# Token mixers of a two-block network: branch order, convolution taps and a reciprocal table

## The chip, the core and the metric

One core of a Trainium2 chip runs the whole program. The metric is the device time of one execution in microseconds, taken as the median of several runs. Five engines work side by side, each through a list of instructions of its own, in order: TensorE (PE, its weight loads are PEld), VectorE (DVE), ScalarE (ACT), GpSimd (POOL) and SyncE (SP, which issues most DMAs). They wait for each other through semaphores.

## What is computed

Two blocks follow each other on 256 tokens of width 1024. The change lies in the first one, which has two layers. Each layer runs a token mixer and a gated feed-forward net; in layer 0 also 256 context tokens go through it (512 columns in all), in layer 1 the 256 tokens alone ask, with keys and values of the context. The mixer has three branches, each closed by a projection and a gate:

```python
u = h @ w_glu                                   # convolution branch, 512 channels
u = u[..., :512] * sigmoid(u[..., 512:])
u = depthwise_conv(u, conv_w, conv_b)           # 31 taps
y_a = silu(layer_norm(u, ln_g, ln_b)) @ w_conv_out

q, k, v = diff_qkv(h, w_q, w_k, w_v)            # 8 heads, two score sets each
p = softmax(q k / 8)                            # both sets
o = (p[:, :, 0] - lam * p[:, :, 1]) @ v
y_b = rms_norm(o) * (1 - lam_init) @ w_attn_out

p = h @ w_p                                     # pool branch, windows 2, 4, 8, 16
y_c = (groupwise(window_mean(p) - p, w_group) * scale) @ w_pool_out

g = sigmoid(h @ w_g + b_gate)                   # three gates of 1024
y = (g[0] * y_a + g[1] * y_b + g[2] * y_c) @ w_out
```

Beside that, `silu(c) @ w_mod + b_mod` gives shifts and scales of every layer, and the second block, which is not touched, starts from an rms norm of 256 memory tokens (`mem_norm`).

## The kernel before

All activations lie transposed, 128 channels by the tokens, in tiles of a common ring (`slot`, SLOTS = 66 tiles of 128x512); the convolution's and the pool's padded inputs have a ring of their own (`u_tile`, US = 6). Each float32 product is made as three matmuls of split operands, hi by hi, hi by lo and lo by hi (`mm3`, L164 to L166). A weight piece is loaded by SP, ScalarE writes its high part (`whi`, L154) and VectorE, for some pieces GpSimd, subtracts the low part (`wlo`, L155); four pieces of each may be in use. PSUM has six buffers for products (`p`) and two for transposes and small sums (`tr`).

`mixer1` (L747) makes a list of steps, each with a cost. `merge(main, side)` spreads the side steps evenly over the main ones by cost, and `emit` runs the list in that order. This order is the priority of a scheduler, which then sorts the instructions of each engine by when their inputs and buffers are due; a step that needs no new buffer can come earlier than its place, one that takes a slot hardly can.

The steps of a mixer in the kernel before, by the stages of which the text speaks:
- projections of the gated convolution input, then queries, keys and values of head pair 0, with the first 20 of 124 convolution taps beside them;
- four attention stages: the projections of the next head pair (in the fourth: the gate of the convolution branch, `gates(0)`) merged with the attention of the current pair (`att_s` scores and softmax, `att_t` transposes, `att_v` values) and 26 taps each. A tap (`conv_tap`) of channel tiles 0 and 1 is one VectorE instruction (L795), one of tiles 2 and 3 a scaling on ScalarE into a slot (L792) and an addition on GpSimd (L793). The first 62 taps belong to tiles 0 and 2 (the first group), the others to tiles 1 and 3 (the second);
- `o_fin`, which finishes the heads' scale factors; the pool projection (4 tiles) merged with the layer norm of the convolution, `conv_ln` (sums), `conv_ln2` (root and broadcast), `conv_ln3` (four tiles);
- `b1`, the convolution's output product (8 tiles, evacuated on VectorE by `merge_a`, L947), merged with the window sums (`pool_win`);
- `gates(2)`, the gate of the pool branch, in layer 0 merged with the first seven parts of a modulation product that VectorE makes (`mod_v`, L476 and L478, its weights `mraw` loaded half a megabyte at a time into two buffers), in layer 1 with `mem_norm(0)`;
- `groups`, the pool's small group products (L1010, L1011 evacuate them), and `b3`, its output product, added by `merge_c` (L952, addition on GpSimd L953);
- `b2`, the attention's gate and output products in turn, with the transposes of the finished heads (`o_tr`, L1031 to L1035) at its start and the rest of the modulation behind; then the mixer's output product.

`att_s` takes the reciprocals of both softmax sums into a small tile (L856) and copies the first of them into a table V["Ri"] (L860), where `o_fin` finds it.

## Time and profile before

| | us |
|---|---|
| median of 3 runs | 2349.7 |
| the runs | 2348.4, 2349.7, 2353.44 |
| span of the profiled execution | 2355.8 |
| TensorE busy | 2197.7 (93%) |
| VectorE busy | 1707.7 (72%) |
| ScalarE busy | 1095.3 (46%) |
| GpSimd busy | 536.5 (23%) |

The profile shows one execution; its span is 6.1 us longer than the median. The mixer of layer 0 lies at about 107 to 610 us, that of layer 1 at 1117 to 1431 us. In the tables of stages, TensorE's idle time is the length of a stage less TensorE's busy time, and PEclk is the clock that TensorE was granted as a share of the full one (2.4 GHz; 0.5 of it is the lower level of 1.2 GHz). Idle time of the other engines costs nothing as long as TensorE does not wait for them.

### The profile page before, as it was taken

What the parts mean: (1) busy time and instruction counts of PE and PEld (TensorE: products, weight loads), DVE (VectorE), ACT (ScalarE), POOL (GpSimd) and SP (SyncE); (2) the same over time, 40 slices, a digit from 0 to 9 for tenths busy, and PEclk for the clock granted to TensorE, in tenths of its full rate; (3) what the DMA queues carried; (4) which work ended last, traced back from release to release, by engine and by line L of the source; (5) the groups of instructions that cost most, each with busy time, mean ns of one, the idle gap of its engine ahead of it and who ended that gap; (6) DMA issues with size and microseconds to landing.
All of it is one profiled execution on the core that took longest, in us unless ns stands there. A gap on an engine that the chain in (4) does not pass through costs nothing.

```text
span 2355.8 us, 37801 instructions
## 1 busy us (share of the span) xinstructions
PE 2197.7 (93%) x14576; PEld 1998.8 (85%) x14576; DVE 1707.7 (72%) x3443; ACT 1095.3 (46%) x2110; POOL 536.5 (23%) x545
## 2 busy tenths in 40 slices
PE   4978889999989999989999899999889999999998
PEld 3767777788888888878788899999877999988998
DVE  5697987959678745578988877764686766686665
ACT  5436565332332222244566554554446544465543
POOL 2344433321340110143333312100342000210000
PEclk8989999999999999998999999999987999999999
DMA  7312112335414555553322454455541555542553
GB/s 271 93 55 67 54 59 72 123 132 170 152 63 154 168 179 170 170 165 108 108 72 90 148 174 160 154 193 176 160 90 37 176 183 177 177 144 84 185 180 125
DMA packets 296628, 319.21 MB, mean 135 GB/s; under 512 B 20544, under 2 KB 264352, under 8 KB 296448
## 3 DMA queue, kind: packets, MB, share of 16 engines
q1 hardware_dynamic: 293072, 311.27, 41.1%
q0 software_dynamic: 2224, 3.43, 0.6%
q8 instruction: 114, 1.87, 0.3%
q10 hardware_dynamic: 1152, 2.10, 0.3%
q14 instruction: 66, 0.54, 0.1%
HBM read 315.72 MB, written 1.05 MB: 134 GB/s over the span
## 4 chain that ended last, share of the span: by engine, by line
PE 66%; DVE 21%; issue 4%; ACT 3%; DMA 3%; POOL 1%; SPq 0%; ACTq 0%; DVEq 0%; POOLq 0%
PE p L164 19%; PE p L165 19%; PE p L166 19%; DVE wlo L155 3%; DVE t L795 3%; DVE t L478 2%; DVE t L258 2%; PE p L742 1%; DVE b L851 1%; DMA mraw<-in_w_mod_dram 1%; DVE t L725 1%; PE tr L484 1%; DMA raw<-in_w_in_dram 1%; PE p L247 1%; ACT whi L154 1%
## 5 line engine op out<-in xcount | busy, mean ns | idle before, releaser
L164 PE MATMUL p<-t,whi 128*128 128x256 f32 (+1 forms) x3724 | 1175.5, 320 | 20.8 <-ACT t L560 8.5
L165 PE MATMUL p<-t,whi 128*128 128x256 f32 (+1 forms) x3724 | 1183.0, 319 | 5.6 <-DVE t L561 2.1
L166 PE MATMUL p<-t,wlo 128*128 128x256 f32 (+1 forms) x3724 | 1178.2, 318 | 6.4 <-DVE wlo L155 4.8
L164 PEld LDWEIGHTS p<-t,whi 128*128 128x128 f32 x3724 | 718.8, 195 | 72.6 <-ACT t L560 10.3
L165 PEld LDWEIGHTS p<-t,whi 128*128 128x128 f32 x3724 | 723.6, 194 | 50.8 <-DVE t L659 3.5
L166 PEld LDWEIGHTS p<-t,wlo 128*128 128x128 f32 x3724 | 723.1, 194 | 50.4 <-DVE wlo L155 5.9
L154 ACT ACTIVATE whi<-raw 128x1024 fp32r<-128x1024 f32 (+4 forms) x487 | 492.0, 1020 | 543.4 <-PE p L165 332.6
L155 DVE TENSOR_TENSOR wlo<-raw,whi 128x1024 fp32r<-128x1024 f32 (+4 forms) x443 | 545.4, 1232 | 201.7 <-ACT whi L154 113.7
L155 POOL TENSOR_TENSOR wlo<-raw,whi 128x1024 fp32r<-128x1024 f32 (+2 forms) x44 | 103.5, 2353 | 503.6 <-ACT whi L154 464.8
L478 DVE SCALAR_TENSOR_TENSOR t<-mraw,big,t 128x512 f32<-128x512 f32 x224 | 176.6, 827 | 17.7 <-DMA mraw<-in_w_mod_dram 16.2
L793 POOL TENSOR_TENSOR t<-t,t 128x512 f32<-128x512 f32 (+1 forms) x120 | 134.9, 1125 | 186.0 <-ACT t L792 178.5
L594 POOL TENSOR_TENSOR t<-t,t 128x256 f32<-128x256 f32 (+1 forms) x68 | 70.4, 1063 | 246.1 <-ACT t L596 242.8
L299 POOL TENSOR_TENSOR t<-t,t 128x256 f32<-128x256 f32 (+1 forms) x27 | 25.6, 948 | 430.6 <-ACT t L297 430.1
L260 ACT ACTIVATE t<-t 128x256 fp32r<-128x256 f32 (+1 forms) x115 | 54.3, 473 | 148.9 <-DVE t L689 104.4
L742 PE MATMUL p<-t,t 64*128 64x256 f32 (+2 forms) x528 | 78.5, 374 | 28.5 <-DVE t L261 9.8
L247 PE MATMUL p<-whi,t 128*128 128x256 f32 x352 | 101.8, 289 | 2.8 <-ACT t L853 1.6
L248 PE MATMUL p<-wlo,t 128*128 128x256 f32 x352 | 99.8, 284 | 0.0
L249 PE MATMUL p<-whi,t 128*128 128x256 f32 x352 | 99.8, 283 | 0.0
L689 DVE TENSOR_TENSOR t<-t,p 128x256 f32<-128x256 f32 (+1 forms) x91 | 43.1, 474 | 76.8 <-PE p L166 76.6
L795 DVE SCALAR_TENSOR_TENSOR t<-u,big,t 128x512 f32<-128x512 f32 (+1 forms) x120 | 94.9, 791 | 1.5
L742 PEld LDWEIGHTS p<-t,t 64*128 64x128 f32 x528 | 50.9, 206 | 49.2 <-issue 16.8
L257 ACT ACTIVATE t<-t 128x256 fp32r<-128x256 f32 (+1 forms) x92 | 43.2, 495 | 100.0 <-DVE t L725 80.6
(299 smaller groups left out, 2717.0 us busy)
## 6 DMA issues: line engine op xcount, KB each, us to landing
raw<-in_w_in_dram SPq DMA_DIRECT2D x60, 1024.0 KB, 5.1
raw<-in_l_w_gate_up_dram SPq DMA_DIRECT2D x44, 1024.0 KB, 5.1
raw<-in_w_ffn_in_dram SPq DMA_DIRECT2D x42, 1024.0 KB, 5.3
mraw<-in_w_mod_dram SPq DMA_DIRECT2D x80, 512.0 KB, 4.0
raw<-in_l_w_in_dram SPq DMA_DIRECT2D x15, 1024.0 KB, 5.2
raw<-in_l_w_down_dram SPq DMA_DIRECT2D x16, 896.0 KB, 4.9
t<-in_w_mod_dram SPq DMA_DIRECT2D x32, 256.0 KB, 5.4
raw<-in_w_attn_out_dram SPq DMA_DIRECT2D x8, 1024.0 KB, 5.2
```

The source lines that it names most:

```text
L154: nc.scalar.activation(p.hi, src, AF.Copy)
L155: eng.tensor_tensor(p.lo, src, p.hi, op=ALU.subtract)
L164: mm(ps, lh, rh, start=first, stop=False)
L165: mm(ps, lh, rl, start=False, stop=False)
L166: mm(ps, ll, rh, start=False, stop=last)
L247: mm(ps[:, :256], lh, p.hi[:, k % 4], start=k == 0, stop=False)
L248: mm(ps[:, :256], lh, p.lo[:, k % 4], start=False, stop=False)
L249: mm(ps[:, :256], ll, p.hi[:, k % 4], start=False, stop=k == 7)
L478: nc.vector.scalar_tensor_tensor(acc, w[:, k], c, acc, op0=ALU.mult, op1=ALU.add)
L742: self.nc.tensor.matmul(out[half], q[i // 2][h, qs], k[i % 2][h, ks], start=i == 0, stop=i == 2)
L793: nc.gpsimd.tensor_tensor(acc, acc, t, op=ALU.add)
L795: nc.vector.scalar_tensor_tensor(acc, u, w, acc, op0=ALU.mult, op1=ALU.add)
```

## The change

The three branches are added in another order, pool first, then convolution, then attention, and the side steps stand beside other main steps. The first addition (now of the pool) writes V["m"], the convolution's adds to it on GpSimd, the attention's still comes last. The gates' tiles are keyed by branch, since two gates are now alive together. The attention stages get 17, 17, 17 and 23 taps, the fourth has `gates(2)` beside it; 11 taps each go beside the pool projection and the first four tiles of `gates(0)`, the rest beside the pool's output product. The softmax reciprocals are written straight into a table of twice the size and the copy goes.

```diff
-SLOTS, RING, MORE, RAWS, US, MRAWS = 66, 4, 4, 2, 6, 2
+SLOTS, RING, MORE, RAWS, US, MRAWS = 64, 4, 4, 2, 7, 2
...
-        V["Ri"] = self.const([128, 8 * nq], self.nm("Ri"))
+        V["Ri"] = self.const([128, 16 * nq], self.nm("Ri"))
...
-            r = self.brief([128, 2])
+            j = hd * nq + t
+            r = V["Ri"][:, 2 * j:2 * j + 2]
             nc.vector.reciprocal(r, L)
...
-            j = hd * nq + t
-            nc.vector.tensor_copy(V["Ri"][:, j:j + 1], r[:, 0:1])
...
-            V["gt", m] = t
+            V["gt", br, m] = t
...
-        def merge_a(m, ps):
-            t = V.pop(("gt", m))
+        def merge_c(m, ps):
+            t = V.pop(("gt", 2, m))
...
             V["m", m] = t
-        def merge_c(m, ps):
-            t = V.pop(("gt", m))
+        def merge_a(m, ps):
+            t = V.pop(("gt", 0, m))
...
-        out += merge(qkv(0), conv[:20])
-        ncv = len(conv) - 20
+        taps = iter(conv)
+        take = lambda n: [t for _, t in zip(range(n), taps)]
+        out += merge(qkv(0), take(17))
         for pr in range(4):
-            main = qkv(pr + 1) if pr < 3 else gates(0)
-            side = att(pr)
-            out += merge(merge(main, side), conv[20 + pr * ncv // 4: 20 + (pr + 1) * ncv // 4])
-        out.append(X(o_fin))
+            main = qkv(pr + 1) if pr < 3 else gates(2)
+            out += merge(merge(main, att(pr)), take(17 if pr < 3 else 23))
         pl = []
         self.lin(pl, W, 4096, 512, hx, N, pool_evac)
+        out += merge(pl, take(11) + [X(o_fin)])
+        rest = [X(lambda m=m: pool_win(m)) for m in range(4)]
+        if l == 1:
+            rest.append(X(lambda: self.mem_norm(0)))
+        g0 = gates(0)
+        out += merge(merge(g0[:4], rest), take(11))
+        gr = groups()
+        b3 = []
+        self.lin(b3, a["w_pool_out"][l], 0, 1024, lambda: V["z"], N, merge_c, K=4)
+        out += gr + merge(b3, list(taps))
         side = [X(conv_ln), X(conv_ln2)] + [X(lambda m=m: conv_ln3(m)) for m in range(4)]
-        out += merge(pl, side)
+        out += merge(g0[4:], side, 1)
         b1 = []
         self.lin(b1, a["w_conv_out"][l], 0, 1024, lambda: V["u3"], N, merge_a, K=4)
-        out += merge(b1, [X(lambda m=m: pool_win(m)) for m in range(4)])
+        ms = []
         if l == 0:
-            ms = []
             self.mod_v(ms, 0, (4, 5, 8, 9, 6, 7), 2)
-            out += merge(gates(2), ms[:8])
-        else:
-            out += merge(gates(2), [X(lambda: self.mem_norm(0))])
-        out += groups()
-        b3 = []
-        self.lin(b3, a["w_pool_out"][l], 0, 1024, lambda: V["z"], N, merge_c, K=4)
-        out += b3
+        out += merge(b1, ms[:12])
...
-        out += merge(b2[:2], [X(lambda h=h: o_tr(h)) for h in range(8)]) + (merge(b2[2:], ms[8:]) if l == 0 else b2[2:])
+        out += merge(b2[:2], [X(lambda h=h: o_tr(h)) for h in range(8)]) + merge(b2[2:], ms[12:])
```

Outside the two mixers the order of every engine stays. Inside, three places are shown as the scheduler leaves them. Comments are removed too, so that line numbers differ by one or two.

VectorE at the end of the third attention stage of layer 0, before. L155 is a weight subtraction, L258 the low half of a value tile, L887 the reduction of a finished head, L795 a tap, and L851 the row maxima of the fourth stage's first scores:

```order
L155 TENSOR_TENSOR wlo_3153<-raw,whi_3152 128x1024
L258 TENSOR_TENSOR t_3137<-p_3112,t_3137 128x2x128
L887 TENSOR_REDUCE t_2991<-tr_3143 128x128
L795 SCALAR_TENSOR_TENSOR t_2269<-u_802,big,t_2269 128x512
L155 TENSOR_TENSOR wlo_3242<-raw,whi_3241 128x1024
L851 TENSOR_REDUCE b_1313<-p_3192 128x1
L851 TENSOR_REDUCE b_1313<-p_3193 128x1
L851 TENSOR_REDUCE b_1313<-p_3210 128x1
L851 TENSOR_REDUCE b_1313<-p_3211 128x1
L856 RECIPROCAL b_1313<-b_1313 128x2
```

The same place in the changed kernel (L886 is the reduction):

```order
L155 TENSOR_TENSOR wlo_3069<-raw,whi_3068 128x1024
L258 TENSOR_TENSOR t_3053<-p_3028,t_3053 128x2x128
L886 TENSOR_REDUCE t_2912<-tr_3059 128x128
L795 SCALAR_TENSOR_TENSOR t_2841<-u_802,big,t_2841 128x512 x7
L851 TENSOR_REDUCE b_1305<-p_3107 128x1
L851 TENSOR_REDUCE b_1305<-p_3108 128x1
L851 TENSOR_REDUCE b_1305<-p_3125 128x1
L851 TENSOR_REDUCE b_1305<-p_3126 128x1
```

Before, one tap stands between the reduction and the maxima, and the taps end soon after; now seven stand there, and more of the second group's follow in the fourth stage, while the first group's in the first stage keep their places.

VectorE in layer 0, where the first split of the transposed heads (L1035) comes, before. L952 is the last merge of the pool product:

```order
L952 SCALAR_TENSOR_TENSOR t_4457<-t_4457,p_4630 128x512
L155 TENSOR_TENSOR wlo_4646<-raw,whi_4645 128x1024
L155 TENSOR_TENSOR wlo_4749<-raw,whi_4748 128x1024
L1035 SCALAR_TENSOR_TENSOR t_4677<-tr_4692,big,t_4676 128x512
L1035 SCALAR_TENSOR_TENSOR t_4679<-tr_4703,big,t_4678 128x512
L1035 SCALAR_TENSOR_TENSOR t_4681<-tr_4714,big,t_4680 128x512
L1035 SCALAR_TENSOR_TENSOR t_4683<-tr_4725,big,t_4682 128x512
L1035 SCALAR_TENSOR_TENSOR t_4685<-tr_4736,big,t_4684 128x512
```

The same in the changed kernel. L951 is the merge of a convolution output tile, L478 a modulation multiply and add on `mraw` weights:

```order
L951 SCALAR_TENSOR_TENSOR t_4409<-t_4409,p_4618 128x512
L155 TENSOR_TENSOR wlo_4640<-raw,whi_4639 128x1024
L478 SCALAR_TENSOR_TENSOR t_4586<-mraw_4612,big,t_4586 128x512
L478 SCALAR_TENSOR_TENSOR t_4587<-mraw_4612,big,t_4587 128x512
```

and further on, behind five more of L478:

```order
L478 SCALAR_TENSOR_TENSOR t_4587<-mraw_4633,big,t_4587 128x512
L1035 SCALAR_TENSOR_TENSOR t_4671<-tr_4686,big,t_4670 128x512
L1035 SCALAR_TENSOR_TENSOR t_4673<-tr_4697,big,t_4672 128x512
L155 TENSOR_TENSOR wlo_4743<-raw,whi_4742 128x1024
L155 TENSOR_TENSOR wlo_4807<-raw,whi_4806 128x1024
L1035 SCALAR_TENSOR_TENSOR t_4675<-tr_4708,big,t_4674 128x512
```

Before, merges and weight subtractions alone stand ahead of the splits; now 38 of L478 and 6 of L476 stand between the last convolution normalisation and the first L1035.

ScalarE in layer 1, ahead of the evacuation of the pool groups, before. L909 is a gate tile, L1010 the groups' evacuation:

```order
L909 ACTIVATE t_12866<-p_12841,big 128x256
L154 ACTIVATE whi_12868<-raw 128x1024
L154 ACTIVATE whi_12900<-raw 128x1024
L909 ACTIVATE t_12897<-p_12872,big 128x256
L1010 ACTIVATE t_12904<-p_12908,big 128x256
L1010 ACTIVATE t_12904<-p_12914,big 128x256
L154 ACTIVATE whi_12932<-raw 128x1024
L1010 ACTIVATE t_12906<-p_12920,big 128x256
L1010 ACTIVATE t_12906<-p_12926,big 128x256
```

The same in the changed kernel. L908 is the gate tile, L792 the scaling of a tap, L1308 the squares of the memory tokens, L1330 the high halves of the normalised memory, L1009 the groups' evacuation:

```order
L908 ACTIVATE t_12397<-p_12372,big 128x256
L792 ACTIVATE t_12399<-u_9853,big 128x256
L154 ACTIVATE whi_12528<-raw 128x1024
L1308 ACTIVATE t_12412,c_12411<-t_12403 128x512
L1308 ACTIVATE t_12414,c_12411<-t_12405 128x512
L1308 ACTIVATE t_12416,c_12411<-t_12407 128x512
L1308 ACTIVATE t_12418,c_12411<-t_12409 128x512
L1330 ACTIVATE t_12471<-t_12448,big 128x256 x2
L1330 ACTIVATE t_12473<-t_12455,big 128x256 x2
L1330 ACTIVATE t_12475<-t_12462,big 128x256 x2
L1330 ACTIVATE t_12477<-t_12469,big 128x256 x2
L1009 ACTIVATE t_12500<-p_12504,big 128x256
L1009 ACTIVATE t_12500<-p_12510,big 128x256
```

The memory normalisation has come between the gate tile and the groups' evacuation. On VectorE its sums, scalings, copies and low halves stand ahead of the groups' low halves in the same way, and on GpSimd its four loads stand behind the tap that adds the output of the L792 above.

## Rows read from the trace of the kernel before

**Rows 1.** The page: its head, and the chain that ended last, by engine.

```profile
span 2355.8 us, 37801 instructions
...
PE 66%; DVE 21%; issue 4%; ACT 3%; DMA 3%; POOL 1%; SPq 0%; ACTq 0%; DVEq 0%; POOLq 0%
```

**Rows 2.** Layer 0 windows: us, busy PE, PEld, DVE, ACT, POOL, then PEclk, DMA, GB/s.

```profile
140.40:211.60 71.20, 52.84 (x315) 44.05 (x314) 61.32 (x119) 37.21 (x90) 29.58 (x22) 0.88 0.17 55
211.60:268.40 56.80, 50.66 (x314) 42.66 (x313) 47.52 (x107) 33.80 (x85) 24.62 (x18) 0.97 0.18 57
268.40:328.20 59.80, 51.78 (x315) 43.36 (x314) 58.61 (x119) 35.16 (x91) 23.51 (x18) 0.97 0.16 54
328.20:387.40 59.20, 58.40 (x310) 46.52 (x309) 36.04 (x71) 35.59 (x82) 21.52 (x14) 1.00 0.22 72
387.40:439.40 52.00, 48.38 (x216) 38.01 (x215) 48.91 (x104) 20.77 (x34) 24.95 (x23) 1.00 0.23 75
439.40:482.90 43.50, 43.50 (x193) 36.03 (x192) 37.73 (x48) 13.13 (x17) 5.39 (x2) 1.00 0.58 184
```

**Rows 3.** Windows of line L795 alone: us, VectorE busy (count), PEclk, DMA, GB/s.

```profile
140.40:211.60 71.20, 19.37 (x19) 0.88 0.17 55
268.40:328.20 59.80, 19.25 (x21) 0.97 0.16 54
```

**Rows 4.** TensorE's timeline: start, us, work, the idle time before and its releaser.

```profile
153.64 1.01 PE L742 MATMUL p<-t,t 64*128 64x256 f32 x3 [5.99 <-DVE t L258]
161.61 0.98 PE L742 MATMUL p<-t,t 64*128 64x256 f32 x3 [6.96 <-DVE t L261]
```

**Rows 5.** Timelines of VectorE and then GpSimd in layer 0's first stage.

```profile
143.16 2.23 DVE L795 SCALAR_TENSOR_TENSOR t<-u,big,t 128x512 f32<-128x512 f32 x2
...
167.28 0.74 DVE L795 SCALAR_TENSOR_TENSOR t<-u,big,t 128x512 f32<-128x512 f32 x1
...
139.35 4.70 POOL L793 TENSOR_TENSOR t<-t,t 128x512 f32<-128x512 f32 x3 [1.49 <-ACT t L792]
```

**Rows 6.** VectorE's timeline, one row; then groups: count, busy us, mean ns, idle.

```profile
455.15 4.90 DVE L478 SCALAR_TENSOR_TENSOR t<-mraw,big,t 128x512 f32<-128x512 f32 x7
...
L155 DVE TENSOR_TENSOR wlo<-raw,whi 128x1024 fp32r<-128x1024 f32 x363 | 461.5, 1273 | 144.2 <-ACT whi L154 90.1 <-PE p L166 43.5 <-issue 5.0
...
L953 POOL TENSOR_TENSOR t<-t,t 128x512 f32<-128x512 f32 x8 | 10.3, 1292 | 12.6 <-DVE t L952 12.6
...
L860 DVE COPY big<-b 128x1 f32<-128x1 f32 x48 | 6.9, 144 | 0.0
```

**Rows 7.** Windows of layer 1, with the columns of rows 2.

```profile
1149.10:1194.00 44.90, 39.69 (x267) 35.08 (x266) 39.95 (x85) 24.61 (x58) 13.82 (x18) 0.96 0.22 71
1232.50:1275.90 43.40, 39.61 (x266) 35.00 (x266) 40.09 (x85) 24.95 (x60) 13.30 (x18) 0.96 0.23 74
1275.90:1309.70 33.80, 32.65 (x266) 30.73 (x265) 23.77 (x42) 25.77 (x57) 11.47 (x13) 1.00 0.37 125
1309.70:1343.60 33.90, 27.60 (x205) 26.61 (x204) 31.77 (x91) 15.68 (x31) 13.08 (x25) 0.90 0.39 126
1343.60:1368.90 25.30, 25.11 (x212) 24.91 (x211) 22.29 (x54) 16.68 (x33) 0.00 (x0) 1.00 0.53 176
```

**Rows 8.** Line L1301, its landing; timelines of VectorE and ScalarE behind it.

```profile
L1301 POOL DMA_DIRECT2D t<-in_mem_dram x4: 543/548/621, 1336.5 to 1338.1; - x4
...
DMA to landing us min/median/max: 3.1/3.5/4.1
...
1351.88 0.16 DVE L1308 TENSOR_REDUCE c<-c 128x2 f32<-128x4 f32 x1 [0.45 <-ACT t L1306]
...
1356.09 1.68 DVE L1313 TENSOR_SCALAR t<-t,c 128x512 f32<-128x512 f32 x4
...
1351.14 0.61 ACT L1306 ACTIVATE t<-t 128x512 f32<-128x512 f32 x1
...
1359.53 3.57 ACT L1328 ACTIVATE t<-t,big 128x256 fp32r<-128x256 f32 x8 [2.75 <-DVE t L1322]
```

More of the change, by code (lines that the diff above doesn't have):

```diff
@@ L889, in att_v @@
             sq = self.slot()
-            nc.scalar.activation(sq[:, :128], o, AF.Square, scale=V["Ri"][:, j:j + 1], accum_out=V["SS"][:, j:j + 1])
+            nc.scalar.activation(sq[:, :128], o, AF.Square, scale=V["Ri"][:, 2 * j:2 * j + 1], accum_out=V["SS"][:, j:j + 1])
         def att(pr):
@@ L955, in merge_b @@
         def merge_b(m, ps):
-            t = V.pop(("gt", m))
+            t = V.pop(("gt", 1, m))
             nc.vector.scalar_tensor_tensor(t[:, :N], t[:, :N], 1.0, ps[:, :N], op0=ALU.add, op1=ALU.mult)
@@ L1020, in o_fin @@
             r = self.rsqrt(v, 8 * nq)
-            nc.vector.tensor_tensor(V["Ri"], r, V["Ri"], op=ALU.mult)
+            ri = V["Ri"].rearrange("p (j i) -> p j i", i=2)[:, :, 0]
+            nc.vector.tensor_tensor(ri, r, ri, op=ALU.mult)
         def o_tr(hd):
@@ L1030, in o_tr @@
                 j = hd * nq + t
-                nc.vector.tensor_scalar(o[:, s], o[:, s], V["Ri"][:, j:j + 1], None, op0=ALU.mult)
+                nc.vector.tensor_scalar(o[:, s], o[:, s], V["Ri"][:, 2 * j:2 * j + 1], None, op0=ALU.mult)
                 nc.tensor.transpose(ps[:, s], o[:, s], self.ident)
```

## The prediction

> **What bounds the kernel now.** I read the page first: the profiled execution has a span of 2355.8 us, and the chain that ended last is 66% TensorE and 21% VectorE [rows 1]. TensorE is therefore the bound, and a change pays only where TensorE waits. So the second view is the table of stages, for the two places that the change moves: the token mixers of layer 0 and layer 1 of the first block. In layer 0 the reader is to see that the three stages with attention beside projections leave TensorE idle for 18.4, 6.1 and 8.0 us (length less busy time), that VectorE is 98% busy in the third, and that the fourth, attention beside a gate, loses almost nothing while VectorE is at 36.0 of 59.2 us [rows 2]. The convolution taps, L795, are what fills VectorE: 19 of them take 19.4 us of the first stage and 21 take 19.3 us of the third [rows 3]. The third view is TensorE's own timeline at the worst place: two holes of 6.0 and 7.0 us in the first stage, both ended by VectorE's evacuation of a projection (L258, L261), which stood behind taps [rows 4]. The last view is VectorE beside GpSimd there: a tap alone takes 0.74 us; two take 2.23 us while GpSimd adds, so the hindered one cost about 0.65 us more [rows 5].
>
> The span lies 6.1 us above the median of the runs, 2349.7 us. I make the sum against the span and take 6.1 us off at the end.
>
> **The change part by part, layer 0.**
> Stage 1 (attention of heads 0 and 1): the order shows the taps of the first channel group on VectorE in their old places; only the GpSimd ones thin, by six up to the stage's end. Six times 0.65 us [rows 5] is 3.9 us of VectorE on the path of the holes: **−4** (−1 if the evacuations still come last behind the VectorE taps, −8 if ScalarE's six fewer scalings help too).
> Stages 2 and 3: the second group's VectorE taps leave them for the end of stage 3 and for stage 4. Idle time there is 6.1 + 8.0 us, and a granted clock of 0.97, between TensorE's levels of 1.2 and 2.4 GHz, hides some 3.5 us more in 116.6 us [rows 2]. With some 16 of the 19.3 us of taps gone [rows 3], VectorE has about 43 us of work in stage 3, under TensorE's 51.8. The softmax chain and the rotations still wait on each other, so not all of the 17.6 us comes back: **−11** (−6 to −14).
> Stage 4: it receives some 26 taps. At 0.74 us to 1.0 us they are 19 to 26 us on a VectorE that has 36.0 busy, so 55 to 62 us against TensorE's 58.4 [rows 2]. Taps fill gaps, but an evacuation can stand behind a run of seven: **+3.5** (0 to +10).
> Pool, normalisation of the convolution, its product (387.4 to 439.4): 192 large matmuls at the price of the gate stage (43.5 us for 193, all busy) are 43.3 us, some 24 small ones about 3 us more; the two stages took 52.0 [rows 2]. The normalisation chain, which now lies beside four gate tiles and the pool product instead of beside the short pool projection alone, loses its 5.5 us of exposure: **−5** (−6, or +2 if the last taps come late).
> Modulation beside the convolution's product: this is the new wait. Before, seven parts of the modulation product stood beside the last gate, whose evacuations are ScalarE's. Now eleven stand beside the convolution's product, whose evacuations are VectorE's, and the order puts 44 instructions of them ahead of the first split of the transposed heads (L1035), for which TensorE's second pair of head transposes waits. VectorE has to do 44 × 0.70 + 8 merges of the same size × 0.70 + 3 weight subtractions × 1.27 = 40.2 us, and 8 additions on GpSimd of 1.29 us hinder it by some 0.65 us each, 5.2 us; two splits make 46.8 [rows 5, 6]. TensorE has 144 large matmuls and eight transposes before it needs them, 33.5 us at the gate stage's price [rows 2]. The difference is 13; the scalings that open a group are cheaper than the 0.70 and some parts start early: **+11** (+5 without any hindrance, +17 if the modulation weights also land late). The remaining parts, fewer than before, lie beside a stage that TensorE fills: nothing, and nothing is lost if that cover is gone, as they were there already.
>
> **Layer 1**, with half the columns. Stage 1 idles 5.2 us; fewer GpSimd taps give **−1** (0 to −2). Stage 3 idles 3.8 us at a clock of 0.96, some 5.5 us together, and most of it goes with the taps: **−5** (−2 to −6), stage 2 included. Stage 4 has 23.8 of 33.8 us of VectorE busy and gets 20 taps of half the width, about 0.55 us each by estimate from the 0.74 to 1.0 us above: 35 against 33.8: **+3** (0 to +6) [rows 7].
> Pool to convolution product: 33.9 us. At the price of the gate stage behind it (25.1 us for 212 matmuls) the 192 large ones are 22.8, the small ones 2.5; 8.6 us are lost, to idle time and to a clock of 0.90 [rows 7]. They go: **−8** (−5 to −8.6).
> Memory normalisation: before, it stood beside a whole gate, and that stage lost 0.2 us [rows 7]. Now its four loads stand on GpSimd's queue behind a tap that waits for the fourth gate tile, and its ScalarE and VectorE steps stand ahead of the evacuation of the pool groups on both engines, so TensorE's pool product waits for the whole chain. From the end of the fourth gate tile: some 1.7 us, an estimate, for that evacuation and the tap's scaling and addition; 4 × 0.55 us of issue; 3.5 us to landing; the last square, 0.6 us; 2.2 us for the sum and root (4.2 us between the rows, less a weight subtraction and a wait); 1.7 us of scaling; 1.2 us for a transpose and copy; 3.6 us for the eight ScalarE splits [rows 8]. That is 16.7 us, less some 2.6 us that the groups' evacuation would take by itself: **+14**, and about 2.5 us at the lower clock after such a hole, as in the 0.90 stretch: **+16.5** (+8, if the scheduled order lets the loads go ahead, to +19).
>
> **Copies.** 48 of 0.144 us leave VectorE, 32 in layer 0 [rows 6]; 6.9 us of busy time, of which what lies in stages that VectorE holds counts: **−1** (0 to −4). One more buffer for the padded tiles and two fewer of the common ones: nothing on the rows read here waits for a buffer of either kind; 0 (−1 to +2). Which branch adds first: the same instructions, 0.
>
> **Sum.** Layer 0: −4 − 11 + 3.5 − 5 + 11 = −5.5. Layer 1: −1 − 5 + 3 − 8 + 16.5 = +5.5. Copies −1. The span becomes 2354.8, the time 2354.8 − 6.1 = 2348.7; I say **2348.5 us**. A measurement of this kernel tells 0.2% (4.7 us) from no change, so the forecast is no difference that can be told: two reliefs paid back at two new waits.
>
> One rule of the Trainium skill speaks against moving the memory loads. What rows show: the four issues on GpSimd took 0.543 to 0.621 us each [rows 8]. The Trainium skill's page "SBUF — State Buffer", section "A bandwidth-pool intuition that's wrong (but worth ruling out)", says that a DMA whose descriptors GpSimd writes takes about 3.1 us instead of 0.62 us when VectorE holds the port that the two share. [...]
>
> **The rivals.**
> 1. The relief is larger. The holes of stage 1 [rows 4] close because the thinner taps leave ScalarE and GpSimd in time, so that the stage comes as near to its matmuls as stage 2 does: 71.2 to about 61, −10 instead of −4; and stage 4 takes its taps for nothing in both layers, −6.5. Together −12.5: **2336 us**. For it: TensorE idles 18.4 us there. Against it: the taps named in rows 3 don't move in that stage.
> 2. Stage 4 becomes bound by VectorE in both layers: the moved taps meet GpSimd's additions at 1.4 us instead of 0.74 us [rows 5]. It decides from the point where VectorE's work exceeds the 58.4 us of TensorE; 26 such taps make 36 + 36 = 72 at the worst, of which I price +10 and +6 instead of 3.5 and 3: **2358 us**. For it: one tap in two ran hindered in stage 1. Against it: GpSimd's taps thin as well, and a tap has no due time.
> 3. The memory loads are held up where they are issued: VectorE has a row of weight subtractions queued there, and if each of the four issues has to wait for two of them, of 1.27 us [rows 6], the chain of layer 1 grows by 4 × 2.5 us: **2358.5 us**. It decides if an issue takes over 1.8 us. For it: GpSimd and VectorE hinder each other in rows 5. Against it: the four issues of before stay at 0.621 us at most [rows 8].
> 4. The change doesn't spread what it says: stage 1 gains nothing since its VectorE taps stay, **2352.5 us**.
>
> **How the numbers follow.** The forecast has 0.42 (0.28 within 0.2%, 0.08 below, 0.06 above), rival 1 0.28, rival 2 0.15, rival 3 0.08, rival 4 0.07. Faster: 0.08 + 0.28 = 0.36. Same: 0.28 + 0.07 = 0.35. Slower: 0.06 + 0.15 + 0.08 = 0.29. The forecast's own range is 2341 to 2356; with both signs likely, the range for all reaches from rival 1's lower side to a little above rivals 2 and 3, 2333 to 2362.
>
> **What would show it.** In the table of stages after: layer 0's stage 1 still over 65 us and its two holes still there; stage 3 some 8 us shorter with VectorE under 50; stage 4 a few us longer. A hole of TensorE of 5 to 17 us in layer 0 ahead of the second pair of head transposes, ended by L1035, and one of 8 to 16 us in layer 1 ahead of the pool product, ended by the evacuation of the groups. If the second hole is missing, the order on the chip let the loads run early, and the time falls to about 2335; if stage 1 shrinks by 10, rival 1 holds; if the issues take over 1.8 us each, rival 3.

## The result and the profile after

The changed kernel takes 2385.84 us (2384.19 to 2389.32), 1.0143 of the kernel before, interval 1.0119 to 1.0166: 34 us slower, where 1 us less had been forecast. In a second comparison, beside its copy with another buffer number, it gave 1.0143 again (1.0123 to 1.0163).

The head of the page and the chain by engine, which answer to [rows 1]:

```profile
span 2382.4 us, 37700 instructions
...
PE 66%; DVE 19%; ACT 5%; issue 4%; DMA 3%; POOL 2%; SPq 0%; ACTq 0%; DVEq 0%; POOLq 0%
```

VectorE's part of the chain has fallen from 21% to 19% and ScalarE's has risen from 3% to 5%. The stages of layer 0, cut at the same TensorE instructions as in [rows 2] up to 384.1 us; behind that the stages are new ones (pool projection and four tiles of the convolution's gate; pool groups and product; the other four tiles and the convolution's product; the attention's gate and product). Columns as there:

```profile
144.10:210.20 66.10, 52.13 (x316) 43.74 (x315) 56.98 (x110) 33.22 (x84) 21.62 (x16) 0.90 0.16 53
210.20:264.70 54.50, 49.76 (x313) 42.70 (x312) 38.27 (x89) 32.13 (x84) 19.60 (x15) 0.97 0.18 59
264.70:318.30 53.60, 49.13 (x316) 41.56 (x315) 45.53 (x99) 31.39 (x83) 15.66 (x12) 1.00 0.19 60
318.30:384.10 65.80, 60.48 (x308) 48.03 (x307) 53.84 (x85) 34.91 (x80) 21.96 (x13) 0.95 0.20 65
384.10:428.40 44.30, 44.30 (x199) 36.56 (x198) 34.73 (x63) 19.52 (x33) 31.56 (x29) 1.00 0.23 78
428.40:461.50 33.10, 27.62 (x110) 21.49 (x109) 21.78 (x23) 14.82 (x22) 20.36 (x12) 0.90 0.30 96
461.50:515.30 53.80, 50.62 (x227) 40.71 (x226) 46.45 (x68) 17.50 (x25) 13.31 (x7) 0.97 0.33 101
515.30:625.20 109.90, 101.65 (x484) 84.72 (x483) 93.67 (x133) 31.46 (x40) 16.44 (x8) 0.97 0.56 181
```

The first three stages are 5.1, 2.3 and 6.2 us shorter than before, the fourth 6.6 us longer. The two holes of [rows 4] in the first stage are still there:

```profile
155.70 1.01 PE L742 MATMUL p<-t,t 64*128 64x256 f32 x3 [4.38 <-DVE t L258]
...
163.79 0.98 PE L742 MATMUL p<-t,t 64*128 64x256 f32 x3 [7.09 <-DVE t L261]
```

Then the loss begins: TensorE is idle 5.5 us in the stretch of the pool groups, 3.2 us in the next and 8.3 us in the last one. In the kernel before, the pool groups and product, and the attention's gate and product, had taken:

```profile
482.90:509.50 26.60, 26.60 (x125) 21.88 (x125) 13.46 (x16) 8.44 (x11) 13.31 (x9) 1.00 0.35 118
509.50:610.00 100.50, 99.52 (x493) 83.54 (x491) 83.64 (x117) 32.00 (x40) 12.17 (x6) 1.00 0.52 162
```

The same for layer 1 of the changed kernel, against [rows 7] (the stretch from 1316.8 to 1340.0 us, pool projection and four gate tiles, has no idle time and is left out):

```profile
1160.00:1203.30 43.30, 40.01 (x268) 35.32 (x267) 38.75 (x82) 22.86 (x53) 9.03 (x13) 0.96 0.23 74
1203.30:1241.40 38.10, 38.10 (x267) 33.91 (x266) 29.23 (x61) 23.00 (x53) 10.46 (x13) 1.00 0.26 84
1241.40:1279.50 38.10, 38.10 (x267) 33.90 (x266) 33.70 (x73) 21.33 (x52) 9.64 (x11) 1.00 0.26 84
1279.50:1316.80 37.30, 34.25 (x264) 32.02 (x264) 33.74 (x57) 24.48 (x55) 10.03 (x11) 0.95 0.34 112
1340.00:1382.10 42.10, 20.80 (x126) 18.58 (x125) 26.14 (x57) 18.78 (x38) 9.80 (x13) 0.68 0.32 104
1382.10:1412.60 30.50, 26.48 (x208) 25.01 (x207) 24.43 (x56) 14.61 (x26) 11.65 (x13) 1.00 0.38 123
```

Half of the 42.1 us of the pool groups and product is idle, at a mean granted clock of 0.68. From the start of the first attention stage to the last addition of the attention's branch, the mixer of layer 0 takes 482.8 us instead of 470.4 and that of layer 1 301.2 instead of 282.2: the attention stages give 7.0 and 3.8 us, and what follows them costs 19.4 and 22.8. TensorE's timeline names the larger holes (start, length, work, idle time and its releaser), four in layer 0 and five in layer 1:

```profile
435.23 0.79 PE L164 MATMUL p<-t,whi 128*128 128x512 f32 x1 [4.72 <-ACT t L257]
506.66 1.05 PE L484 MATMUL tr<-big,t 128*128 128x1 f32 x8 [2.47 <-DVE t L478]
529.65 0.50 PE L164 MATMUL p<-t,whi 128*128 128x512 f32 x1 [1.40 <-DVE t L951]
537.76 1.12 PE L1032 MATMUL tr<-big,t 128*128 128x128 f32 x4 [6.48 <-DVE t L1035]
1344.55 0.38 PE L164 MATMUL p<-t,whi 128*128 128x256 f32 x1 [2.74 <-ACT t L257]
1348.54 0.58 PE L164 MATMUL p<-t,whi 128*128 128x256 f32 x1 [2.93 <-ACT t L257]
1360.75 3.95 PE L1321 MATMUL tr<-big,t 128*128 128x128 f32 x16 [10.39 <-DVE t L1315]
1368.49 0.80 PE L164 MATMUL p<-t,whi 128*128 128x256 f32 x2 [3.80 <-ACT t L1009]
1386.88 0.70 PE L924 MATMUL tr<-t,big 128*128 128x256 f32 x2 [2.01 <-DVE t L922]
```

The hole at 537.76 waits for the split of the transposed heads (L1035), those at 1360.75 and 1368.49 for the memory normalisation and the groups behind it; both had been forecast. Those at 506.66 and 529.65 wait for the modulation itself (L478) and for a merge of the convolution's product beside it (L951), that at 1386.88 for the normalisation of the convolution. Those at 435.23, 1344.55 and 1348.54 had not been forecast: they wait for the split (L257) of a pool window. What makes it late is seen on GpSimd and VectorE in layer 0, ahead of the first of these holes. The first fence is the kernel before, the second the changed one:

```profile
425.31 13.35 POOL L984 TENSOR_TENSOR u<-u 128x570 f32<-128x570 f32 x8 [6.20 <-DVE t L990]
```

```profile
415.18 13.16 POOL L983 TENSOR_TENSOR u<-u 128x570 f32<-128x570 f32 x8
...
413.24 0.68 DVE L989 TENSOR_TENSOR t<-u,t 128x512 f32<-128x512 f32 x1
417.23 1.63 DVE L989 TENSOR_TENSOR t<-u,t 128x512 f32<-128x512 f32 x1
418.90 1.51 DVE L990 TENSOR_TENSOR t<-t,u 128x512 f32<-128x512 f32 x1
...
428.29 5.62 POOL L793 TENSOR_TENSOR t<-t,t 128x512 f32<-128x512 f32 x3
...
431.04 1.75 DVE L989 TENSOR_TENSOR t<-u,t 128x512 f32<-128x512 f32 x1
```

Eight window sums in a row take GpSimd 13.2 us, as long as before; but they began 57 us ahead of the stretch of the pool groups before, and begin 13 us ahead of it now. VectorE's steps on the windows take 1.5 to 1.6 us beside them, 0.68 us ahead of them. The last window's steps, behind the sums, are as slow: GpSimd adds three taps there, of those that the change has put beside the windows.

In layer 1 the memory's loads stand behind the windows and the taps. In order of time: a window's split that waits for a tap's addition, the next window's split, the fourth gate tile leaving PSUM (L908), the tap behind it, the loads, the first and the last square:

```profile
1344.08 0.42 ACT L257 ACTIVATE t<-t 128x256 fp32r<-128x256 f32 x1 [3.18 <-POOL t L793]
...
1348.07 0.42 ACT L257 ACTIVATE t<-t 128x256 fp32r<-128x256 f32 x1 [0.92 <-DVE t L990]
1348.39 0.46 ACT L908 ACTIVATE t<-p,big 128x256 f32<-128x256 f32 x1
...
1349.38 0.73 POOL L793 TENSOR_TENSOR t<-t,t 128x256 f32<-128x256 f32 x1 [2.10 <-ACT t L792]
1350.05 2.22 POOL L1303 DMA_DIRECT2D t<-in_mem_dram  x4
...
1352.98 0.63 ACT L1308 ACTIVATE t<-t 128x512 f32<-128x512 f32 x1 [1.75 <-DMA t<-in_mem_dram]
...
1357.18 0.63 ACT L1308 ACTIVATE t<-t 128x512 f32<-128x512 f32 x1 [1.42 <-DMA t<-in_mem_dram]
```

The fourth gate tile ends at 1340.1 us on TensorE, but ScalarE takes it out only at 1348.39, behind the splits of the windows. One of these had waited 3.18 us for a tap's addition; it reads no tap, so what it waited for is the tile that it writes. The loads are issued ten us after the end of the gate tile, and from there to the pool product the memory's chain takes 18.4 us.

### The profile page after: what moved, and what is told of

The parts are those of the page before. It is cut to its first block, busy times and chain, and to the rows that moved or that the text cites. A ratio compares the mean times of both kernels' runs of the same rounds, so it can differ in the third digit from the quotient of the medians.

```text
span 2382.4 us, 37700 instructions
## 1 busy us (share of the span) xinstructions
PE 2199.2 (92%) x14576; PEld 1997.1 (84%) x14576; DVE 1714.1 (72%) x3395; ACT 1097.3 (46%) x2110; POOL 542.8 (23%) x545
## 4 chain that ended last, share of the span: by engine, by line
PE 66%; DVE 19%; ACT 5%; issue 4%; DMA 3%; POOL 2%; SPq 0%; ACTq 0%; DVEq 0%; POOLq 0%
PE p L164 19%; PE p L165 19%; PE p L166 19%; DVE t L795 3%; DVE wlo L155 3%; DVE t L478 2%; DVE t L258 1%; PE p L742 1%; ACT whi L154 1%; PE tr L484 1%; DVE b L851 1%; DVE t L725 1%; PE p L247 1%; PE p L249 1%; PE p L248 1%
## 5 line engine op out<-in xcount | busy, mean ns | idle before, releaser
L155 DVE TENSOR_TENSOR wlo<-raw,whi 128x1024 fp32r<-128x1024 f32 (+4 forms) x443 | 542.8, 1231 | 162.8 <-ACT whi L154 148.0
L155 POOL TENSOR_TENSOR wlo<-raw,whi 128x1024 fp32r<-128x1024 f32 (+2 forms) x44 | 105.2, 2391 | 446.3 <-ACT whi L154 433.1
L478 DVE SCALAR_TENSOR_TENSOR t<-mraw,big,t 128x512 f32<-128x512 f32 x224 | 180.4, 847 | 14.2 <-DMA mraw<-in_w_mod_dram 12.5
L795 DVE SCALAR_TENSOR_TENSOR t<-u,big,t 128x512 f32<-128x512 f32 (+1 forms) x120 | 93.3, 778 | 1.9
L257 ACT ACTIVATE t<-t 128x256 fp32r<-128x256 f32 (+1 forms) x92 | 43.2, 495 | 109.6 <-DVE t L725 86.2
```

The source lines that it names most:

```text
L155: eng.tensor_tensor(p.lo, src, p.hi, op=ALU.subtract)
L478: nc.vector.scalar_tensor_tensor(acc, w[:, k], c, acc, op0=ALU.mult, op1=ALU.add)
L795: nc.vector.scalar_tensor_tensor(acc, u, w, acc, op0=ALU.mult, op1=ALU.add)
```

## Experiments: the three late waits

Theory: three waits make the loss, the memory's chain, the pool windows without cover, and the modulation ahead of the head transposes. Each was cured alone in the changed kernel. The difference of two such ratios is known to about 7 us either way, so gains of 12 and 14 us can't be told apart; beside them stands what the traces show of the stretch behind the attention stages.

**The memory's chain.** In layer 1 it goes beside the convolution's product.

```diff
-        if l == 1:
-            rest.append(X(lambda: self.mem_norm(0)))
...
+        else:
+            ms.append(X(lambda: self.mem_norm(0)))
```

> The changed kernel, with the memory normalisation of layer 1 moved from the first four gate tiles to the convolution's output product, so that it no longer stands ahead of the evacuation of the pool groups. In the changed kernel's trace TensorE stands for 21 us in four holes between the fourth gate tile (ends at 1340.1 us) and the pool product (starts at 1368.5 us); the loads of the memory are issued only at 1350.05 us. Theory: two chains follow each other there, first the pool windows (1340 to 1350, about 10 us), then the memory's (1350 to 1368.5, about 18 us); without the second the pool product starts some 16 to 18 us earlier, and the time falls by 14 to 18 us against the changed kernel, 1.0143 to about 1.007 to 1.008. Rival: the pool windows alone hold TensorE, and the memory's work only fills the time of that wait: then under 5 us are gained.

Measured 1.0082 (1.0059 to 1.0105), 14 us less than the changed kernel; 12.4 us in the trace, in layer 1. The pool windows' holes stay (2.1 and 2.8 us at 1345.2 and 1349.4 us), the 10.39 us hole is gone, and the chain makes two smaller ones in its new place:

```profile
1398.22 0.44 PE L1321 MATMUL tr<-big,t 128*128 128x128 f32 x2 [3.18 <-DVE t L1315]
1405.99 0.62 PE L164 MATMUL p<-t,whi 128*128 128x256 f32 x3 [4.53 <-ACT t L1034]
```

The rival falls.

**The pool windows.** The sums move to VectorE.

```diff
-                nc.gpsimd.tensor_tensor(nx[:, :nseg, lo_:hi_], cur[:, :nseg, lo_ + da:hi_ + da],
+                nc.vector.tensor_tensor(nx[:, :nseg, lo_:hi_], cur[:, :nseg, lo_ + da:hi_ + da],
```

> The changed kernel, with the window sums of the pool branch added on VectorE instead of GpSimd (20 additions in all). Theory: the pool product waits because the windows, which had two stages of cover before, now have four gate tiles, and GpSimd makes them one after the other at 1.6 us (layer 0) while each slows VectorE's own steps from 0.7 to 1.5 us and more; on VectorE the ten sums of a layer take some 7 us (layer 0) and 4 us (layer 1), and the hole ahead of the pool product goes: layer 0 loses its 4.7 us hole and the slow clock behind it, 5 to 6 us; in layer 1 the memory loads, queued behind the windows on GpSimd, are issued some 6 to 9 us earlier. Together 10 to 14 us against the changed kernel, ratio 1.0085 to 1.010. Rival: it is ScalarE's order (its split stands behind weight splits and gate tiles) that paces the windows; then the holes stay and less than 4 us are gained.

Measured 1.0091 (1.0069 to 1.0113), 12 us less; 3.0 us in the trace in layer 0 and 3.5 in layer 1. The 4.72 us hole of layer 0 has become 1.19 and 0.90 us, but in layer 1, where two holes made 5.7 us, one of 4.66 us for a window's split is left beside one of 0.95 us: the engine is a part of the matter and not all of it.

```profile
426.46 0.49 PE L164 MATMUL p<-t,whi 128*128 128x512 f32 x1 [1.19 <-ACT t L257]
1343.36 0.58 PE L164 MATMUL p<-t,whi 128*128 128x256 f32 x1 [4.66 <-ACT t L257]
```

**The modulation.** Six parts instead of eleven stand beside the convolution's product.

```diff
-        out += merge(b1, ms[:12])
+        out += merge(b1, ms[:6])
...
- ... + merge(b2[2:], ms[12:])
+ ... + merge(b2[2:], ms[6:])
```

> The changed kernel, with six instead of eleven modulation parts of layer 0 beside the convolution's output product; the other five go behind the head transposes, where 18 parts then stand (17 in the kernel before). Theory: VectorE's queue ahead of the split of the transposed heads shrinks from 47 to about 31 us, under TensorE's 33.5 us, so the holes of 2.5, 1.4 and 6.5 us there go with the slow clock behind them: 9 to 12 us less than the changed kernel, ratio about 1.0095 to 1.0105, and nothing is lost later, since the kernel before carried 17 parts there. Rival: VectorE is the bound over both stages together, so that the time comes back later: under 3 us gained.

Measured 1.0085 (1.0064 to 1.0106), 14 us less. In the trace it is 6.5 us, in layer 0. The 2.47 us hole is gone, and the 6.48 us hole is split into one of 2.26 us and three about 1 us; the rest of it is not paid back later.

```profile
520.17 0.50 PE L164 MATMUL p<-t,whi 128*128 128x512 f32 x1 [2.26 <-ACT t L1034]
```

**The spread of the taps**, undone alone in the changed kernel (20 and 26 taps as before).

```diff
-        out += merge(qkv(0), take(17))
+        out += merge(qkv(0), take(20))
...
-            out += merge(merge(main, att(pr)), take(17 if pr < 3 else 23))
+            out += merge(merge(main, att(pr)), take(26))
```

> The changed kernel, with the convolution taps in the old numbers, 20 beside the first projections and 26 in each attention stage, none later. Theory: the spread of the taps is what relieved the attention stages (12 us in layer 0's first three stages and 9 in layer 1's, of which 8 came back in the fourth); undone, these stages get longer by about 12 us; the later stages have no taps beside the pool windows and gain up to 6 us: 6 us slower than the changed kernel, ratio about 1.0165 to 1.018. Rival: the taps beside the pool windows are what makes the holes ahead of the pool product; then the later stages gain more than the early ones lose, and the ratio is under 1.012.

Measured 1.0139 (1.0117 to 1.0160): no difference from the changed kernel, between the two theories. The trace shows both halves: in layer 0 the third attention stage is 10.5 us longer and the fourth 4 to 6 us shorter, by where it is cut; what follows the attention stages is 7.3 us shorter in layer 0 and 8.8 us in layer 1. As the rival says, the taps beside the windows are part of what makes the holes: the sums are still GpSimd's, yet TensorE is never idle around the pool groups of layer 0 (the first line), and in layer 1 1.11 us are left ahead of the groups instead of 5.67.

```profile
424.00:456.00 32.00, 32.00 (x141) 26.17 (x140) 22.34 (x26) 12.74 (x18) 11.33 (x8) 1.00 0.39 132
...
1357.47 0.39 PE L164 MATMUL p<-t,whi 128*128 128x256 f32 x1 [1.11 <-ACT t L257]
```

**All three cures**, the memory later still, beside the last half of the attention's gates and products; the sums go to VectorE as above.

```diff
-        if l == 1:
-            rest.append(X(lambda: self.mem_norm(0)))
-        out += merge(b1, ms[:12])
+        out += merge(b1, ms[:6])
...
- ... + merge(b2[2:], ms[12:])
+ ... + (merge(b2[2:], ms[6:]) if l == 0 else b2[2:8] + merge(b2[8:], [X(lambda: self.mem_norm(0))]))
```

> The changed kernel with all three cures: the window sums on VectorE, six modulation parts beside the convolution's output product, and the memory normalisation of layer 1 beside the last half of the attention's gates and products. Theory: the three losses are separate, 14.3, 12.2 and 13.6 us in the runs of each alone, less some 6 us that the first two share in layer 1, plus some 6 us for a better place of the memory's chain, which left holes of 3.2 and 4.5 us beside the convolution's product: about 40 us less than the changed kernel, ratio 0.996 to 0.999. Rival: cured of one wait TensorE meets the next one, and the sum is under 25 us: ratio over 1.003.

Measured 1.0037 (1.0021 to 1.0053), 25 us less than the changed kernel: the sum of the three holds only in part, as the rival had it, and the kernel is still slower than the one before. What follows the attention stages is nearly as short as before in layer 1 (122.4 us to the last addition of the attention's branch; 121.6 before, 144.4 in the changed kernel). In layer 0 it is not (228.8 us; 220.0 before, 239.4 in the changed kernel):

```profile
425.50:510.00 84.50, 80.77 (x355) 64.90 (x354) 66.06 (x89) 32.92 (x45) 33.79 (x20) 0.98 0.33 106
510.00:611.60 101.60, 96.21 (x466) 79.40 (x464) 92.11 (x132) 30.26 (x39) 14.40 (x6) 0.98 0.58 184
```

VectorE is busy for 92.1 of the last 101.6 us, where TensorE has 96.2 us to do; moved back, the modulation meets an engine that is nearly full. That this is what holds the kernel back was not tried apart.

**All cures with the old taps**: the diff of the taps above, `take(17)` to `take(20)` and `take(17 if pr < 3 else 23)` to `take(26)`, in the kernel with all three cures.

> The kernel with all three cures, but the convolution taps in the old numbers (20, then 26 in each attention stage). Theory: the spread of the taps relieves the attention stages by about 12 us, and in the run with the old numbers alone this was paid back since the windows then had GpSimd for themselves; with the windows on VectorE nothing is paid back: 6 to 12 us slower than the kernel with all three cures. Rival: the spread only moves taps from one stage to another, and the two kernels differ by less than 4 us.

Measured 1.0079 (1.0049 to 1.0109), 10 us slower than with the new taps: here the relief of the attention stages is not paid back, as the theory said.

**Cover for the windows.** The sums are back on GpSimd; the pool projection and the windows go into the fourth attention stage, and the cures of the modulation and the memory stay. Buffers 66 and 8.

```diff
-SLOTS, RING, MORE, RAWS, US, MRAWS = 64, 4, 4, 2, 7, 2
+SLOTS, RING, MORE, RAWS, US, MRAWS = 66, 4, 4, 2, 8, 2
...
-            main = qkv(pr + 1) if pr < 3 else gates(2)
-            out += merge(merge(main, att(pr)), take(17 if pr < 3 else 23))
-        out += merge(pl, take(11) + [X(o_fin)])
+            main = qkv(pr + 1) if pr < 3 else pl + merge(gates(2), rest)
+            out += merge(merge(main, att(pr)), take(17 if pr < 3 else 34))
...
-        out += merge(merge(g0[:4], rest), take(11))
+        out += merge(g0[:4], [X(o_fin)] + take(11))
```

> The kernel with the cures for the modulation and the memory, the window sums back on GpSimd, but with the pool projection moved ahead into the fourth attention stage and the windows beside its gate, so that they have that gate and four more gate tiles as cover (buffer numbers 66 and 8, 34 taps in that stage). Theory: cover is what the windows lack in the changed kernel, whatever engine sums them: the hole ahead of the pool product goes, and the ratio is like that of the kernel with all three cures or up to 5 us better. Rival: the shared port is the matter; then VectorE's taps and evacuations of the fourth stage are slowed by 20 window sums, that stage grows by 8 us or more, and the kernel is slower than the one with all three cures by about as much.

Measured 0.9997 (0.9980 to 1.0014), 9 us less than with the sums on VectorE. No hole before a pool group is left in layer 0, and the fourth stage with the pool projection in it takes 89.45 us, where the kernel with all three cures needs 87.6 us for the two: with cover the sums can stay on GpSimd.

```profile
315.57:405.02 89.45, 83.05 (x410) 66.69 (x409) 76.60 (x102) 47.89 (x102) 46.86 (x38) 0.98 0.19 62
```

The hole ahead of layer 0's pool groups has thus gone or shrunk under three cures, sums on the other engine, no taps beside the windows, and cover; what the windows lacked was time on GpSimd and VectorE ahead of the groups. How much of the 9 us the other buffer numbers and the place of `o_fin` give was not tried apart. This is the best version found, and it equals the kernel before.

## Experiments: the small edits

The prediction had priced the copies at −1 us and the buffer numbers at 0. Both together in the kernel before:

```diff
-SLOTS, RING, MORE, RAWS, US, MRAWS = 66, 4, 4, 2, 6, 2
+SLOTS, RING, MORE, RAWS, US, MRAWS = 64, 4, 4, 2, 7, 2
...
-            r = self.brief([128, 2])
+            j = hd * nq + t
+            r = V["Ri"][:, 2 * j:2 * j + 2]
...
-            nc.vector.tensor_copy(V["Ri"][:, j:j + 1], r[:, 0:1])
```

> The kernel before, with the small edits alone: the softmax reciprocals written straight into the doubled table (48 copies of 0.144 us less on VectorE) and the buffer numbers 64 and 7. Theory: the copies lie in waits of VectorE or beside TensorE's work, and no buffer of either kind is waited for: 0 to 3 us faster, ratio 0.9985 to 1.000. Rival: two buffers less hold the scheduler's early steps back and part of the loss of the change comes from there: ratio over 1.002.

Measured 1.0040 (1.0026 to 1.0054): the rival's ratio. My next theory was the scheduler's order without the copies; so they were put back as dead weight:

```diff
+            nc.vector.tensor_copy(self.brief([128, 1]), r[:, 0:1])
```

> The kernel before with the small edits (reciprocals straight to the table, 64 and 7 buffers), which alone were 0.40% slower, and the 48 copies put back as dead weight: they write a tile that nobody reads. Theory: it is not the copies' own time and not the buffers that cost 9 us; without the copies the scheduler sorts VectorE and TensorE otherwise in layer 0's second and third attention stage (a tap or a value tile's evacuation earlier by some places). With the dead copies TensorE, ScalarE and GpSimd have the order of the kernel before again: ratio 0.9985 to 1.0015. Rival: writing and reading the table in strides of two, or the wait of the reciprocal, costs the time: the ratio stays at 1.003 or more.

Measured 1.0055 (1.0035 to 1.0075): that theory fell. The buffer numbers alone:

```diff
-SLOTS, RING, MORE, RAWS, US, MRAWS = 66, 4, 4, 2, 6, 2
+SLOTS, RING, MORE, RAWS, US, MRAWS = 64, 4, 4, 2, 7, 2
```

> The kernel before with 64 common tiles and 7 padded ones instead of 66 and 6, and nothing else. The order of the instructions on every engine is that of the kernel before. Theory: no difference, ratio 0.999 to 1.001; then the whole 0.40% of the small edits belongs to the copies. Rival: other addresses or buffers matter: over 1.002.

Measured 1.0056 (1.0036 to 1.0076): all of the loss. The instructions of every engine stand in the same order as before, but for one weight subtraction of GpSimd, which falls behind two window sums of layer 0 (what follows the attention stages there is no longer, 219.6 us against 220.0); what differs is whose release a tile waits for. With 64 and 6 the waits of the program are those of the kernel before, with 66 and 7 those of this run, so it is the seventh padded tile. Its third attention stage, which took 59.80 us in [rows 2], and the one wait of ScalarE for GpSimd in it that the kernel before does not have there (who waited for whom, us in total, times, longest):

```profile
271.60:336.90 65.30, 55.95 (x315) 46.90 (x314) 61.00 (x120) 35.70 (x91) 24.26 (x18) 0.90 0.15 49
...
ACT t L853 <- POOL t L793: 3.7, 3, 1.8
```

The exponentials of the softmax (L853) now write into tiles that a tap's addition on GpSimd has just read, and wait for it three times. Of the 5.5 us, 1.3 are idle time of TensorE and 4.2 its busy time, at a mean granted clock of 0.90 instead of 0.97. That these waits start it is read off the trace and was not tried. The copies alone, which is the first diff of this section without its first two lines (66 and 6 stay):

> The kernel before, with the reciprocals written straight to the doubled table and the 48 copies gone, and the old buffer numbers (66 and 6). Theory: the number of padded tiles alone made the 0.40% to 0.56% of the three kernels with the small edits; without it the copies' absence is worth 0 to 3 us: ratio 0.9985 to 1.001. Rival: without the copies the scheduler's order of layer 0's attention stages is worse, whatever the buffers: 1.002 to 1.005.

Measured 1.0012 (0.9998 to 1.0026): nothing that can be told.

**Six padded tiles in the changed kernel**, first alone:

```diff
-SLOTS, RING, MORE, RAWS, US, MRAWS = 64, 4, 4, 2, 7, 2
+SLOTS, RING, MORE, RAWS, US, MRAWS = 64, 4, 4, 2, 6, 2
```

> The changed kernel with six padded tiles instead of seven, and nothing else. In the kernel before, a seventh alone (the order of the instructions the same on every engine, other waits for the tiles' former users) cost 0.56%, most of it in layer 0's attention stages. Theory: the seventh takes its place from the common tiles, which then come free later, and this costs the changed kernel as much: 9 to 13 us faster than it, ratio 1.009 to 1.0105. Rival: where the waits fall is particular to each kernel's layout and order; the changed kernel, which needs the pool's padded tiles together, gains nothing or loses: 1.013 or more.

Measured 1.0092 (1.0071 to 1.0114), as the theory had it. As the two profiles differed mostly in a stretch with the same program, both kernels, unedited, ran once more on one chip:

> The changed kernel itself, beside its copy with six padded tiles on the same chip. In the two profiles the mixer stages are equal within 1.5 us, and 5.7 of the 7.7 us between the spans lie in the first 130 us, which are the same program. Theory A: the seventh padded tile costs the changed kernel nothing, the 0.5% between the two was the chip and the clock at the start: both ratios within 0.0015 of each other. Theory B: it costs 9 to 13 us here as in the kernel before: ratio 1.013 to 1.015 here, 1.008 to 1.010 for the copy.

> The changed kernel with six padded tiles, beside the changed kernel on the same chip. Theory A: the same ratio as that, within 0.0015. Theory B: 0.004 to 0.0055 less.

Measured 1.0143 (1.0123 to 1.0163) with seven, 1.0100 (1.0083 to 1.0117) with six: theory B, 10 us. Where in the changed kernel they are lost stays open: the profiled executions are 4 us apart, and no stage of the mixers by more than 3 us. With six, layer 1's mixer is 3 us shorter, and the split of a window that had waited 3.18 us for a tap's addition no longer does; layer 0's is 3 us longer.

With six in the kernel with all three cures, whose work tiles go from 64 to 62 with it:

```diff
-SLOTS, RING, MORE, RAWS, US, MRAWS = 64, 4, 4, 2, 7, 2
+SLOTS, RING, MORE, RAWS, US, MRAWS = 62, 4, 4, 2, 6, 2
```

> The kernel with all three cures (windows on VectorE, six modulation parts, memory normalisation late), with 62 common tiles and six padded ones. With 64 and 7 it took 1.0037 of the kernel before. Theory: as the seventh padded tile costs 9 to 13 us, the ratio falls to 0.998 to 1.000. Rival: the same ratio as before, 1.003 to 1.005, since the windows on VectorE need the seventh.

Measured 1.0023 (1.0010 to 1.0036), against 1.0037 with seven: between theory and rival, and not to be told from no difference. Whether the seventh costs less in this kernel is not shown. The copies put back in the kernel with cover, with their own small table:

```diff
-            r = V["Ri"][:, 2 * j:2 * j + 2]
+            r = self.brief([128, 2])
...
+            nc.vector.tensor_copy(V["Ri"][:, j:j + 1], r[:, 0:1])
```

> The kernel in which the modulation, the memory and the windows have cover (0.9997 of the kernel before), with the copies put back as they were, and the table in its old size. Theory: the copies' absence costs the same through the order here, some 5 to 9 us: ratio 0.996 to 0.998, better than both kernels. Rival: the cost of the missing copies belongs to the old order of taps alone, and nothing changes: 0.999 to 1.001.

Measured 1.0007 (0.9994 to 1.0020) against 0.9997: the rival, in keeping with the copies alone.

## Why the prediction was wrong

- **Attention stages of layer 0**: −4, −11 and +3.5 were forecast; −5.1, −8.5 and +6.6 are measured between the same TensorE instructions. The two holes of [rows 4] stayed (4.38 and 7.09 us), as the order had shown. Right in kind, each within its range.
- **Layer 1's attention stages**: −1, −5 and +3 against −1.6, −5.7 (38.1 instead of 38.5 us in the second, 38.1 instead of 43.4 in the third) and +3.5. Right.
- **Modulation, +11**: the hole stood where it was forecast, ended by L1035, and its cure was worth 14 us by the times, 6.5 us in the trace. Right. The other parts cost next to nothing in the changed kernel, as forecast: the holes of 1.40 and 6.48 us are nearly all of the 8.3 us that TensorE is idle there. With all cures, which move five parts back, TensorE is idle 5.4 us of that stretch.
- **Memory, +16.5**: cured, 14 us. The chain has about the forecast length: 15.0 us to its last split and 2.6 us for the groups' evacuation had been put from the issue on, 18.4 us are measured to the pool product. But it was put at the end of the fourth gate tile, as if the loads waited only for that tile's evacuation and tap; the evacuation stood behind the splits of the windows, and the loads came ten us later.
- **Pool windows and the taps beside them: no term at all.** This is the first step that failed. The part on pool, convolution and product followed the convolution's chain out of its poor cover and did not ask what went into it. The windows had stood beside the convolution's product with the pool's gate behind (23.8 and 43.5 us); now they stand beside four gate tiles, 21.8 us in layer 0 and 11.6 in layer 1, together with eleven taps, on the engine whose work slows VectorE. The rows for it were at hand: a hindered tap in [rows 5], and the length of GpSimd's sums in the trace, 13.35 us. Measured: holes of 4.72 us in layer 0 and 5.67 us in layer 1 ahead of the pool groups, and 12 us less with the sums on the other engine.
- **Buffers, 0 (−1 to +2)**: the second step that failed, by 10 us in the changed kernel and 13 us in the kernel before. "Nothing on the rows read here waits for a buffer of either kind" was read from waits as they fall with the old numbers; it says nothing of the waits that another number makes. For the copies −1 was forecast; their run gives 3 us more, which is not told from none.
- **Normalisation of the convolution, −5 in layer 0**: only 0.65 us of hole is left at its sums. Right.
- **Pool to convolution product in layer 1, −8 (−5 to −8.6)**: the third step that failed, in its size. At the price of [rows 7] by which the forecast went, its work takes 25.3 us. The pool projection's half lost nothing any more, but the four gate tiles and the convolution's product take 30.5 us, 5.2 us over that price, with a hole of 2.01 us at the normalisation's sums: of 8.6 us lost before, 3.4 came back. The normalisation's chain holds TensorE up in its new place too.
- **Rivals**: the relief was not larger, stage 1 did gain, and stage 4 did not become bound by VectorE (53.8 of 65.8 us). The loads were not held up: the four issues took 0.543 to 0.621 us as before, though a weight subtraction ran on VectorE during the last two; only the slowest landing grew, from 4.1 to 5.4 us. The Trainium skill's page "SBUF — State Buffer", section "A bandwidth-pool intuition that's wrong (but worth ruling out)", gives its 3.1 us for a load overlapped with a copy on VectorE, and no copy ran there, so that this rule was not put to the test. No rival had the windows or the buffers.

In the traces 31 us of the loss lie in the two mixers. The attention stages give 7.0 and 3.8 us, against 11.5 and 3 forecast; what follows them costs 19.4 and 22.8 us, against 6 and 8.5. These 27.7 us over the forecast lie in the stretches of the windows, the modulation, the memory's late loads and layer 1's normalisation; the cures overlap, as the run with all of them shows, so no exact share is given to each. The 10 us of the seventh tile are not found among them: with six the two mixers together take as long, within 1 us. So the two accounts do not close, and the tile's share of the 34 us stays open.

## What to carry to other kernels

When a chain is moved, list every chain that lies in the stretch it leaves and in the one it enters, and price the cover that each of them loses, on its slowest engine, not only that of the chain one is looking at. A buffer number is an edit with a price of its own: compare the waits that it sets, not the order alone, and run it alone. A relief counts only if the stretch that takes the work has an idle engine for it. The best version only equals the kernel before. With all three cures VectorE is busy for 92.1 of 101.6 us where the modulation lies, so it is likely that no stretch with an idle VectorE was left; that was not shown.

## What had not been expected of the hardware

A wait is not needed for GpSimd to cost VectorE, as the tap in [rows 5] had shown; for the window steps the price is much the same, 1.5 to 1.6 us beside GpSimd's sums instead of 0.68 us. And one wait of 1.8 us at most, three times 3.7 us in all, comes with a stage 5.5 us longer, with a lower mean granted clock (0.90 instead of 0.97).
